# Recurrence gates of a two-layer hybrid block: plain float32 on dense 64x64 blocks in the four quarters of the array

## The chip, the cores and the metric

The kernel runs on one core of a Trainium2 chip. The metric is the device time of one launch, in microseconds (us). All weights are streamed from DRAM during the launch; the host only lays the inputs out.

## What is computed

Two layers work on 256 latent tokens and 256 context tokens (512 columns in all) of width 1024. Each layer normalises its input, sends it through three mixers (a recurrent block A, a gated linear recurrence B, neighbourhood attention C), merges these with gates, and adds a squared-ReLU MLP. The change is in A. Its recurrence needs two gates for each direction `d`; each is a product of the convolved input `xc` with a block-diagonal matrix, in blocks of 64 channels, cut here to what matters:

```python
xc = centred_depthwise_conv(x_in, conv_w, conv_b)            # (B, T, 512)
xb = xc.reshape(B, T, LRU_BLOCKS, LRU_BLOCK)                 # 8 blocks of 64
r = sigmoid(einsum('btni,dnio->dbtno', xb, wa) + ba)         # d = 2 directions
i = sigmoid(einsum('btni,dnio->dbtno', xb, wx) + bx)
log_a = -LRU_C * r * softplus(-lam)
a = exp(log_a); b = sqrt(-expm1(2 * log_a)) * (i * xc)
hf = linear_scan(a[0], b[0], h0f, False); hb = linear_scan(a[1], b[1], h0b, True)
y = (hf + hb) * gelu(gate_in)
```

## The kernel before

Tokens stand in columns, features in partitions. The kernel is a list of pieces: a piece is the products of one streamed 128x1024 weight tile (`raw`, split into a rounded part `whi` and the rest `wlo`, three products for one), and after every few products a piece yields. Between two yields the class `Lanes` issues steps of dependent chains: lane H (mixer B, `hgrn`), lane A (`attention`), lane L (`lru`, the recurrence of A), N and X (norm and modulation). A step names how many yields it waits. The framework then schedules the instructions of each engine by its own estimate of when their inputs are there; what it fixes is each engine's order, which is what the order rows below show.

For each of the four channel groups `j` of a layer the piece `ax` (tiles `pax`) gives the input of A, `fin_conv` makes `xc` of it, the piece `ag` (`pag`) gives the GeLU branch, and then `lru` starts. It splits the weights `gw` (128x512: four 128x128 matrices with zeros off the diagonal blocks) into `lw` and the input `xc` into `lx`, and multiplies three times for each gate:

```python
ws = [two_k("lw", F32R).rearrange("p (a b) -> p a b", b=P) for _ in range(2)]
split(*ws, gw)
split(*xs, xc)
def product(dst, i):
    for n, (a, b) in enumerate(((0, 0), (0, 1), (1, 0))):
        nc.tensor.matmul(dst, lhsT=ws[a][:, i, :], rhs=xs[b], start=(n == 0), stop=(n == 2))
```

So there are eight `lru` chains (two layers, four groups), each with two directions and two gates, `pr` and `pi`, and 512 columns in both layers. Both gates use the one PSUM bank of tag L. Tag H has two banks, which `hgrn` and every second call of `acc4` (the gates `pg` of the merge among them) take in turn. Tiles of 512 float32 come from a ring of 25 (`t2`), larger ones from a ring of 13 (`t4`). GpSimd's queue (POOL) issues the loads of `gw` and of the attention bias.

Other products use a part of the array at a time: `lv` (within `hgrn`) and `pav` (in `attention`) go to two column tiles of 64 in turn, in plain float32; `ada` goes to four column tiles of 32, in plain float32; the scores `sc` of the two heads go to two row tiles of 64, in float32r.

Of the kernel before, what the change touches and what calls it, by code (L numbers as in the profile page):

```python
# [11 lines left out]
F32R = mybir.dt.float32r  # L12
# [7 lines left out]
P = 128  # L20
# [7 lines left out]
HB = 64  # L28
NLEV = 6
# [27 lines left out]
def merge_order(l):  # L57
    # some gates first, while the mixers' chains end
    count = {}
    for part in MERGE[l].split():  # L60
        bi = int(part[0])
        for what in part[1:]:
            i = count.get((bi, what), 0)
            count[bi, what] = i + 1
            yield bi, BRANCH_ORDER[bi], {"g": "gate", "p": "proj"}[what], i
# [35 lines left out]
class Piece:  # L101
    """Products with streamed weights: body(weights) yields after each run of products."""
# [5 lines left out]
class Lanes:  # L108
    """Chains of dependent steps that are issued between the runs of products.

    A step yields the time that the vector engine needs for what it issued, and how many runs more the chain waits."""
# [43 lines left out]
def hybrid_kernel(  # L155
# [67 lines left out]
    def split(hi, lo, src, scale=None, eng=nc.vector):  # L223
        # hi <- rounded part of scale * src, lo <- the rest
# [21 lines left out]
    def mm3_pairs(dsts, ws, x, nk, c0, c1):  # L246
        # two pieces at a time, so that x may still be arriving
# [15 lines left out]
    def layer_scalars():  # L263
# [13 lines left out]
        for l in range(DEPTH):  # L277
            # f = lb + (1 - lb) * (1 + tanh) / 2 as offset and slope
# [40 lines left out]
    def rope_tables(l):  # L319
        # ctab[:, cos|sin, tile, k|q, head, :], with the norm's gains and the scores' scale  # L320
# [8 lines left out]
    mod = [cpool.tile([P, 3, 2, 16], F32, name=f"mod{l}") for l in range(DEPTH)]  # L329

    def modulation_rows():
        # most sections, a row for each feature: the vector engine has time while the tensor engine is busy
# [34 lines left out]
    def last_modulation():  # L367
        # the last section: four groups of columns in four parts of the array
# [55 lines left out]
    def column_sums(parts, n, tag="A"):  # L424
        # sums over the features, one column for each 128 tokens
# [12 lines left out]
    def spread(r, n, tag="A"):  # L438
        # a row of n * 128 columns in every partition
# [14 lines left out]
    def modulated(u, r, a, b, k, s):  # L454
        # u = h * r * a + b in high and low parts
# [29 lines left out]
    def small_rstd(ss, n, temps):  # L485
        # 1 / sqrt(ss / n + eps) for a few columns: a first guess from the exponent, two steps
# [6 lines left out]
        # with x = v * r * r: r * (15 - 10 x + 3 x^2) / 8, but for the factor 3 / 8, then r * (3 - x) / 2 with that factor  # L493
# [14 lines left out]
    def first_half():  # L508
        # the latent stream's norm, before its products are issued
        q_ = lanes.lanes["N"]  # L510
        while len(q_) > 1 and lanes.step("N"):
            pass

# [1 line left out]
    def hgrn(l, j, TF, Q, vtok, sog, ys):  # L515
# [4 lines left out]
        # products over blocks, states of the context stream  # L520
# [9 lines left out]
        # within blocks of 64 tokens, the blocks of a tile side by side  # L530
# [7 lines left out]
        def place(b, src, shift):  # L538
            # blocks in the upper (b = 0) or the lower half of the partitions
# [13 lines left out]
        def mixed(t, hh, c0, n):  # L553
            # [first halves of slot 0 | second halves of slot 1] of the 2*hh blocks in columns c0..c0+n
# [17 lines left out]
        # A^T[s, t] of both directions, level by level  # L572
        Tt = TF[:]
        width = T2
        for lev in range(8):
# [11 lines left out]
            # widen the products to blocks of 2*hh  # L587
# [30 lines left out]
        # final states of the context stream  # L618
# [18 lines left out]
        # outputs, token-major  # L637
# [34 lines left out]
    def attention(l, j, qk, vtok, bias, ys):  # L672
        Tq = T2 if l == 0 else TL
        misc = two_k("misc")
        # normalised keys and queries, token-major: [k | q] of two heads for each 128 tokens
# [23 lines left out]
        # rotary embedding of the latent tokens  # L699
# [48 lines left out]
        def softmax(qt, sc):  # L748
            # both heads at once
# [55 lines left out]
        def applied(qt):  # L805
            # both heads at once, in two parts of the array
# [28 lines left out]
    def lru(l, j, xc, ge, gw, ys):  # L835
# [3 lines left out]
        xs = [two_k("lx", F32R) for _ in range(2)]  # L839
        ws = [two_k("lw", F32R).rearrange("p (a b) -> p a b", b=P) for _ in range(2)]  # L840
        split(*ws, gw)
        split(*xs, xc)
        yield 1.2, 0

        def product(dst, i):
            for n, (a, b) in enumerate(((0, 0), (0, 1), (1, 0))):
                nc.tensor.matmul(dst, lhsT=ws[a][:, i, :], rhs=xs[b], start=(n == 0), stop=(n == 2))
        for d in range(2):
            c = 2 * j + d
            pr_ = psum("L", "pr")  # L850
            product(pr_, 2 * d)
            nc.scalar.activation(rr[:, d], pr_, AF.Tanh, bias=hb[l][0][:, c:c + 1], scale=0.5)
            yield
            pi_ = psum("L", "pi")
            product(pi_, 2 * d + 1)
            nc.scalar.activation(iis[d], pi_, AF.Tanh, bias=hb[l][1][:, c:c + 1], scale=0.5)
# [37 lines left out]
    def fin_query(Tq, Q, p_):  # L894
        # twice the silu
# [5 lines left out]
    def fin_outgate(l, Tq, sog, p_):  # L901
        # the gain over four times (1 + tanh)
# [17 lines left out]
    def fin_gelu(Tq, ge, p_):  # L920
        # twice the tanh GeLU
# [12 lines left out]
    def mixer_pieces(l):  # L934
        T = T2 if l == 0 else TL
        heads = []
        for j in range(4):
# [9 lines left out]
            def opened(nm, m=m, j=j):  # L947
                # tiles of a chain, when its first piece begins
# [613 lines left out]
```

## Time and profile before

| | |
|---|---|
| median of 3 runs | 1526.17 us (1525.85 to 1526.55) |
| the profiled execution's span | 1526.3 us |
| TensorE (PE) busy | 1513.7 us, 99% of the span |
| VectorE (DVE) busy | 1115.9 us, 73% |
| ScalarE (ACT) busy | 735.0 us, 48% |
| GpSimd (POOL) busy | 26.4 us, 2% |
| granted TensorE clock, mean | 0.999 of full |

The profile is of one execution; its span goes from the first to the last instruction and is its time as far as the page tells it. It lies within the three timed runs, 0.1 us over their median. Busy time of PE counts a product from its start to its modelled end, and products overlap, so the time that a product takes from the others is read from start to start in the timeline.

### The profile page before, as it was taken

The page shows a single profiled execution, that of the slowest core. Times are in us where ns is not written, and L with a number is a line of the kernel's source. Part 1 is how long each engine was busy: PE and PEld are TensorE (multiplying, and loading weights), DVE is VectorE, ACT ScalarE, POOL GpSimd, SP SyncE. Part 2 cuts the span into 40 slices and gives each one's busy share as a digit, 9 for nine tenths or more (in the row PEclk, how much of TensorE's full clock was granted, in tenths as well). Part 3 has the DMA queues.
Part 4 walks back from the last instruction along what each step waited for, and adds up shares of the span by engine and source line. Part 5 has one row for each costly group of instructions (what it writes and reads, how often), then busy time and mean ns, then how long its engine had stood idle before and what let it go on. Part 6 is the DMA issues. An engine that isn't in the chain of part 4 may idle for free.

```text
span 1526.3 us, 24145 instructions
## 1 busy us (share of the span) xinstructions
PE 1513.7 (99%) x9554; PEld 1300.8 (85%) x9554; DVE 1115.9 (73%) x2118; ACT 735.0 (48%) x1229; POOL 26.4 (2%) x57
## 2 busy tenths in 40 slices
PE   9999999999999999999999999999999999999999
PEld 4778788878888889888888889888888899999999
DVE  6776768586478898988685856778787856776664
ACT  3457575666333333532322323475766854454442
POOL 0200000020000000000000000000000000000000
PEclk9999999999999999999999999999999999999999
DMA  9413122221273562445463532313313345755553
GB/s 368 146 53 104 56 90 70 70 77 62 91 250 136 187 240 70 171 174 206 139 220 127 204 126 82 133 63 126 104 70 105 109 167 182 274 167 184 186 183 125
DMA packets 61793, 217.36 MB, mean 142 GB/s; under 512 B 7792, under 2 KB 9456, under 8 KB 61680
## 3 DMA queue, kind: packets, MB, share of 16 engines
q1 hardware_dynamic: 59328, 209.88, 39.5%
q0 software_dynamic: 1648, 5.77, 1.2%
q8 instruction: 75, 1.23, 0.3%
q14 instruction: 38, 0.31, 0.1%
q10 hardware_dynamic: 704, 0.17, 0.1%
HBM read 214.74 MB, written 1.05 MB: 141 GB/s over the span
## 4 chain that ended last, share of the span: by engine, by line
PE 96%; DVE 2%; ACT 1%; issue 1%; DMA 0%; SPq 0%; DVEq 0%
PE pd L240 7%; PE pd L242 7%; PE pd L241 7%; PE pf L242 5%; PE pf L240 5%; PE pf L241 5%; PE pg L240 5%; PE pg L241 4%; PE pg L242 4%; PE ptok L1027 3%; PE ptok L1029 3%; PE ptok L1028 3%; PE lv L547 2%; PE pp L241 2%; PE pp L240 2%; PE pp L242 2%
## 5 line engine op out<-in xcount | busy, mean ns | idle before, releaser
L226 ACT CAST whi<-raw 128x1024 fp32r<-128x1024 f32 x296 | 310.3, 1050 | 477.0 <-PE pd L241 157.2
L227 DVE TENSOR_TENSOR wlo<-raw,whi 128x1024 fp32r<-128x1024 f32 x295 | 360.3, 1223 | 151.2 <-ACT whi L226 149.4
L242 PE MATMUL pd<-hhi,wlo 128*128 128x256 f32 (+1 forms) x544 | 177.8, 327 | 0.0
L240 PE MATMUL pd<-hhi,whi 128*128 128x256 f32 (+1 forms) x544 | 177.8, 327 | 0.0
L241 PE MATMUL pd<-hlo,whi 128*128 128x256 f32 (+1 forms) x544 | 177.7, 327 | 0.0
L354 DVE CUSTOM_DVE_ANT_0 junk<-arow,crow 128x1024 bf16<-128x1024 f32 x144 | 173.3, 1219 | 2.2 <-DMA arow<-in_adaw 2.0
L241 PE MATMUL pf<-xlo,whi 128*128 128x256 f32 (+1 forms) x464 | 155.0, 334 | 0.0
L242 PE MATMUL pf<-xhi,wlo 128*128 128x256 f32 (+1 forms) x464 | 155.0, 334 | 0.0
L240 PE MATMUL pf<-xhi,whi 128*128 128x256 f32 (+1 forms) x464 | 155.0, 334 | 0.0
L240 PE MATMUL pg<-xhi,whi 128*128 128x512 f32 (+1 forms) x384 | 131.5, 342 | 0.0
L241 PE MATMUL pg<-xlo,whi 128*128 128x512 f32 (+1 forms) x384 | 129.2, 336 | 0.0
L242 PE MATMUL pg<-xhi,wlo 128*128 128x512 f32 (+1 forms) x384 | 129.2, 336 | 0.0
L1145 DVE SCALAR_TENSOR_TENSOR h<-pd,mod,h 128x256 f32<-128x256 f32 x120 | 54.9, 480 | 81.2 <-PE pd L242 79.2
L241 PEld LDWEIGHTS pd<-hlo,whi 128*128 128x128 f32 x544 | 103.5, 190 | 8.8
L240 PEld LDWEIGHTS pd<-hhi,whi 128*128 128x128 f32 x544 | 103.5, 190 | 8.8
L242 PEld LDWEIGHTS pd<-hhi,wlo 128*128 128x128 f32 x544 | 103.5, 190 | 8.6
L241 PEld LDWEIGHTS pf<-xlo,whi 128*128 128x128 f32 x464 | 88.1, 190 | 8.8
L242 PEld LDWEIGHTS pf<-xhi,wlo 128*128 128x128 f32 x464 | 88.1, 190 | 8.7
L240 PEld LDWEIGHTS pf<-xhi,whi 128*128 128x128 f32 x464 | 88.0, 190 | 8.7
L1027 PE MATMUL ptok<-whi,xhi 128*128 128x512 f32 (+1 forms) x224 | 87.4, 395 | 1.1 <-DVE h L1145 1.1
L1029 PE MATMUL ptok<-wlo,xhi 128*128 128x512 f32 (+1 forms) x224 | 84.4, 377 | 0.0
L1028 PE MATMUL ptok<-whi,xlo 128*128 128x512 f32 (+1 forms) x224 | 84.2, 376 | 0.2 <-DVE xlo L463 0.2
(329 smaller groups left out, 3240.0 us busy)
## 6 DMA issues: line engine op xcount, KB each, us to landing
raw<-in_wpack SPq DMA_DIRECT2D x296, 512.0 KB, 3.5
arow<-in_adaw SPq DMA_DIRECT2D x72, 512.0 KB, 4.7
a<-in_ada0w SPq DMA_DIRECT2D x16, 512.0 KB, 10.4
araw<-in_lastw SPq DMA_DIRECT2D x8, 512.0 KB, 6.3
bias<-in_biasd POOLq DMA_DIRECT2D x7, 512.0 KB, 4.3
h<-in_xT SPq DMA_DIRECT2D x4, 512.0 KB, 5.5
gw<-in_lruw POOLq DMA_DIRECT2D x8, 256.0 KB, 2.9
out<-h SPq DMA_DIRECT2D x8, 128.0 KB, 2.0
```

The costliest lines, as they stand in the source:

```text
L226: nc.scalar.copy(hi, src)
L227: eng.tensor_tensor(out=lo, in0=src, in1=hi.bitcast(F32), op=ALU.subtract)
L240: nc.tensor.matmul(d, lhsT=whi[:, k, :], rhs=xhi, start=(k == 0), stop=False)
L241: nc.tensor.matmul(d, lhsT=whi[:, k, :], rhs=xlo, start=False, stop=False)
L242: nc.tensor.matmul(d, lhsT=wlo[:, k, :], rhs=xhi, start=False, stop=(k == nk - 1))
L354: nc.vector.tensor_tensor_reduce(out=junk, in0=raw, in1=crow[s], scale=1.0, scalar=0.0, op0=ALU.mult, op1=ALU.add, accum_out=section_of(l, ...
L547: nc.tensor.matmul(dst, lhsT=lhs(b), rhs=rhs(b), start=True, stop=True)
L1027: nc.tensor.matmul(dst, lhsT=xhi[:, k, tsl], rhs=whi[:, kk, :], start=(k == 0), stop=False)
L1028: nc.tensor.matmul(dst, lhsT=xlo[:, k, tsl], rhs=whi[:, kk, :], start=False, stop=False)
L1029: nc.tensor.matmul(dst, lhsT=xhi[:, k, tsl], rhs=wlo[:, kk, :], start=False, stop=(k == KD - 1))
L1145: nc.vector.scalar_tensor_tensor(out=h[:, d, sl], in0=p_[:, sl], scalar=mods(l, section, s)[:, d:d + 1], in1=h[:, d, sl], op0=ALU.mult, op ...
```

## The change

The gate weights are stored as dense 64x64 blocks (`gw` is 128x256). Nothing is split any more: the products are plain float32. Each 64x64 block has a quarter of the array, by the partitions it is read from and those it writes to. For the second gate the host stores the two blocks with their halves changed over, so its input must be `xc` with the upper and lower 64 partitions exchanged; two DMAs on GpSimd's queue make that copy, `lxw`. A bank now holds half of each gate: `pr` (tag L) and `pi` (tag H) are two banks that are filled together, and four tanh of 64 partitions each empty them. Comments were taken out of the whole file as well, which is left out here.

```diff
+LB = 64
...
     def lru(l, j, xc, ge, gw, ys):
         Tq = T2 if l == 0 else TL
         rr, tau = four_k("lr"), four_k("ltau")
         iis = [two_k("li"), two_k("li")]
-        xs = [two_k("lx", F32R) for _ in range(2)]
-        ws = [two_k("lw", F32R).rearrange("p (a b) -> p a b", b=P) for _ in range(2)]
-        split(*ws, gw)
-        split(*xs, xc)
-        yield 1.2, 0
-
-        def product(dst, i):
-            for n, (a, b) in enumerate(((0, 0), (0, 1), (1, 0))):
-                nc.tensor.matmul(dst, lhsT=ws[a][:, i, :], rhs=xs[b], start=(n == 0), stop=(n == 2))
+
+        xw = two_k("lxw")
+        blk = slice(0, LB), slice(LB, P)
+        for b in range(2):
+            nc.gpsimd.dma_start(out=xw[blk[b]], in_=xc[blk[1 - b]])
+        yield 0.0, 2
+
+        def products(d, banks):
+
+
+            for b, p_ in enumerate(banks):
+                nc.tensor.matmul(p_[blk[b]], lhsT=gw[blk[b], 2 * d, :], rhs=xc[blk[b]], start=True, stop=True)
+                nc.tensor.matmul(p_[blk[1 - b]], lhsT=gw[blk[b], 2 * d + 1, :], rhs=xw[blk[b]], start=True, stop=True)
         for d in range(2):
             c = 2 * j + d
-            pr_ = psum("L", "pr")
-            product(pr_, 2 * d)
-            nc.scalar.activation(rr[:, d], pr_, AF.Tanh, bias=hb[l][0][:, c:c + 1], scale=0.5)
+            banks = psum("L", "pr"), psum("H", "pi")
+            products(d, banks)
+            for dst, g in ((rr[:, d], 0), (iis[d], 1)):
+                for b in range(2):
+                    o = blk[b ^ g]
+                    nc.scalar.activation(dst[o], banks[b][o], AF.Tanh, bias=hb[l][g][o, c:c + 1], scale=0.5)
             yield
-            pi_ = psum("L", "pi")
-            product(pi_, 2 * d + 1)
-            nc.scalar.activation(iis[d], pi_, AF.Tanh, bias=hb[l][1][:, c:c + 1], scale=0.5)
             nc.scalar.activation(tau[:, d], rr[:, d], AF.Tanh, bias=s8[l][1][:, c:c + 1], scale=s8[l][1][:, c:c + 1])
...
-                    m.gw = two_k("gw").rearrange("p (a b) -> p a b", b=P)
+                    m.gw = two_k("gw")[:, :4 * LB].rearrange("p (a b) -> p a b", b=LB)
...
-    lw = np.zeros((DEPTH, 4, P, 2, 2, P), np.float32)
+    lw = np.empty((DEPTH, 4, P, 2, 2, LB), np.float32)
...
+            rows = b ^ gi
+            lw[:, :, rows * LB:(rows + 1) * LB, :, gi] = w[:, :, :, b].transpose(0, 2, 3, 1, 4)
```

Line numbers differ between the two files (before L547, L746, L1027 to L1029 are L548, L747, L1032 to L1034 of the changed kernel). On PE in layer 0, group 0, first direction (`ptok` are the products of the next group's token piece, `sc` the attention scores), there stood before, with the second gate `pi` some 20 rows further on:

```order
L547 MATMUL lv<-QQ,km 64x64 x8
L1027 MATMUL ptok<-whi,xhi 128x512
L1028 MATMUL ptok<-whi,xlo 128x512
L1029 MATMUL ptok<-wlo,xhi 128x512
L1027 MATMUL ptok<-whi,xhi 128x512
L1028 MATMUL ptok<-whi,xlo 128x512
L1029 MATMUL ptok<-wlo,xhi 128x512
L746 MATMUL sc<-rotT 128x256 x6
L746 MATMUL sc<-kcT,qT 128x256 x6
L847 MATMUL pr<-lx,lw 128x512 x3
L1027 MATMUL ptok<-whi,xhi 128x512
```

Of the changed kernel, the same place:

```order
L548 MATMUL lv<-QQ,km 64x64 x8
L747 MATMUL sc<-rotT 128x256 x6
L747 MATMUL sc<-kcT,qT 128x256 x6
L1032 MATMUL ptok<-whi,xhi 128x512
L1033 MATMUL ptok<-whi,xlo 128x512
L1034 MATMUL ptok<-wlo,xhi 128x512
L1032 MATMUL ptok<-whi,xhi 128x512
L1033 MATMUL ptok<-whi,xlo 128x512
L1034 MATMUL ptok<-wlo,xhi 128x512
L851 MATMUL pr<-xc,gw 64x512
L852 MATMUL pr<-lxw,gw 64x512
L851 MATMUL pi<-xc,gw 64x512
```

The four products of a direction stand together here (the fourth, `pi<-lxw`, is the next row), between full-array products, and the scores moved ahead of the token products.

On PE in layer 1, group 0, first direction, there stood before, with the scores of each query tile in one run of 12 some rows further on:

```order
L547 MATMUL lv<-QQ,km 64x64 x4
L1027 MATMUL ptok<-whi,xhi 128x512
L1028 MATMUL ptok<-whi,xlo 128x512
L1029 MATMUL ptok<-wlo,xhi 128x512
L1027 MATMUL ptok<-whi,xhi 128x512
L1028 MATMUL ptok<-whi,xlo 128x512
L1029 MATMUL ptok<-wlo,xhi 128x512
L847 MATMUL pr<-lx,lw 128x512 x3
```

Of the changed kernel, the end of that stretch (the first of the four products, `pr<-xc`, stands 22 rows ahead of the second):

```order
L1032 MATMUL ptok<-whi,xhi 128x512
L747 MATMUL sc<-rotT 128x256 x3
L747 MATMUL sc<-kcT,qT 128x256
L747 MATMUL sc<-rotT 128x256 x3
L747 MATMUL sc<-kcT,qT 128x256 x5
L1033 MATMUL ptok<-whi,xlo 128x512
L1034 MATMUL ptok<-wlo,xhi 128x512
L1032 MATMUL ptok<-whi,xhi 128x512
L1033 MATMUL ptok<-whi,xlo 128x512
L1034 MATMUL ptok<-wlo,xhi 128x512
L852 MATMUL pr<-lxw,gw 64x512
L851 MATMUL pi<-xc,gw 64x512
```

One direction's four products are in two bursts here, and the scores of the two heads, one after the other before, come in mixed runs (four of one head, four of the other, then in turn).

On POOL's queue, from layer 0 on, there stood before one `gw` and one `bias` in turn. Of the changed kernel, the rows for the last group of layer 0 and the first two of layer 1:

```order
L327 TENSOR_TENSOR ctab<-cst,gf_74 128x64 x16
L973 DMA gw<-in_lruw 128x256
L844 DMA lxw<-xc 64x512 x2
L965 DMA bias<-in_biasd 128x1024
L973 DMA gw<-in_lruw 128x256
L965 DMA bias<-in_biasd 128x1024
L844 DMA lxw<-xc 64x512 x2
L973 DMA gw<-in_lruw 128x256
L965 DMA bias<-in_biasd 128x1024
L844 DMA lxw<-xc 64x512 x2
```

The two copies of a group are queued behind the loads for the next groups.

## Rows read from the trace of the kernel before

**Rows 1.** The page: span, busy time by engine, chain that ended last.

```profile
span 1526.3 us, 24145 instructions
...
PE 1513.7 (99%) x9554; PEld 1300.8 (85%) x9554; DVE 1115.9 (73%) x2118; ACT 735.0 (48%) x1229; POOL 26.4 (2%) x57
...
PE 96%; DVE 2%; ACT 1%; issue 1%; DMA 0%; SPq 0%; DVEq 0%
```

**Rows 2.** Waits of PE, all of nine: total us, times, longest.

```profile
PE pf L253 <- ACT xhi L462: 2.7, 3, 1.1
...
PE ptok L1028 <- DVE xlo L463: 0.2, 1, 0.2
```

**Rows 3.** Timeline of PE, 112.85 to 114 us: start, us, instruction, count.

```profile
113.08 0.85 PE L847 MATMUL pr<-lx,lw 128*128 128x512 f32 x3
113.77 0.39 PE L1027 MATMUL ptok<-whi,xhi 128*128 128x512 f32 x1
```

**Rows 4.** Timeline of PE around a run of `lv`, 101.3 to 103.1 us.

```profile
101.53 0.39 PE L1029 MATMUL ptok<-wlo,xhi 128*128 128x512 f32 x1
101.84 0.69 PE L547 MATMUL lv<-QQ,km 128*64 128x64 f32 x16
102.46 0.50 PE L1027 MATMUL ptok<-whi,xhi 128*128 128x512 f32 x1
102.79 0.39 PE L1028 MATMUL ptok<-whi,xlo 128*128 128x512 f32 x1
```

**Rows 5.** Timeline of PE around four products of `ada`, 24.4 to 25.9 us.

```profile
24.85 0.64 PE L1333 MATMUL ada<-a,cs 128*32 128x256 f32 x8
25.42 0.73 PE L998 MATMUL ptok<-whi,xhi 128*128 128x512 f32 x2
```

**Rows 6.** The same, only what runs between 24.85 and 24.88 us.

```profile
24.85 0.42 PE L1333 MATMUL ada<-a,cs 128*32 128x256 f32 x4
```

**Rows 7.** Timeline of PE around `pav` and the scores, 108 to 112 us.

```profile
108.85 1.90 PE L812 MATMUL pav<-PT,tok 128*64 128x256 f32 x16
110.68 0.97 PE L746 MATMUL sc<-kcT,qT 64*128 64x256 f32 x12
111.59 0.50 PE L1027 MATMUL ptok<-whi,xhi 128*128 128x512 f32 x1
```

**Rows 8.** Timeline of PE where one head's scores stand alone.

```profile
1197.31 0.62 PE L746 MATMUL sc<-rotT 64*128 64x256 f32 x3
1197.77 0.52 PE L746 MATMUL sc<-kcT,qT 64*128 64x256 f32 x3
1198.21 0.38 PE L240 MATMUL pg<-xhi,whi 128*128 128x256 f32 x1
```

**Rows 9.** Timeline of PE: the last product of `pax`, layer 1, group 0.

```profile
991.98 0.40 PE L242 MATMUL pax<-xhi,wlo 128*128 128x512 f32 x1
```

**Rows 10.** Timeline of DVE: the last step of `xc`, same group.

```profile
996.81 0.74 DVE L915 SCALAR_TENSOR_TENSOR xc<-xpre,prb,xc 128x510 f32<-128x510 f32 x1
```

**Rows 11.** DMA issues by line: queue, count, KB each, median us to landing.

```profile
bias<-in_biasd POOLq DMA_DIRECT2D x7, 512.0 KB, 4.3
...
out<-h SPq DMA_DIRECT2D x8, 128.0 KB, 2.0
```

**Rows 12.** Timeline of POOL: the bias of layer 1, group 3.

```profile
1097.57 0.54 POOL L960 DMA_DIRECT2D bias<-in_biasd  x1 [13.88 <-PE kt L623]
```

**Rows 13.** Timeline of DVE: the last step of `xc`, layer 1, group 2.

```profile
1121.69 0.74 DVE L915 SCALAR_TENSOR_TENSOR xc<-xpre,prb,xc 128x510 f32<-128x510 f32 x1
```

**Rows 14.** Instructions of tile `lx`: ns min/median/max, first and last start.

```profile
L226 ACT CAST lx<-xc x8: 602/636/642, 94.6 to 1185.6; 128x512 fp32r<-128x512 f32 x8
L227 DVE TENSOR_TENSOR lx<-xc,lx x8: 673/685/689, 95.4 to 1189.0; 128x512 fp32r<-128x512 f32 x8
```

**Rows 15.** Instructions of tile `pr`, and who waited for it.

```profile
L852 ACT ACTIVATE lr<-pr,hba x16: 687/690/703, 99.2 to 1203.8; 128x512 f32<-128x512 f32 x16
...
  ACT lr L852: 12.1, 7
```

More of the change, by code (lines that the diff above doesn't have):

```diff
@@ L1490, in _lay @@
     a["prm"] = pm
-    lw = np.zeros((DEPTH, 4, P, 2, 2, P), np.float32)
+    lw = np.empty((DEPTH, 4, P, 2, 2, LB), np.float32)
     for gi, nm in enumerate(("lru_wa", "lru_wx")):
-        w = f[nm].reshape(DEPTH, 2, 4, 2, 64, 64)
+        w = f[nm].reshape(DEPTH, 2, 4, 2, LB, LB)
         for b in range(2):
-            lw[:, :, b * 64:(b + 1) * 64, :, gi, b * 64:(b + 1) * 64] = w[:, :, :, b].transpose(0, 2, 3, 1, 4)
-    a["lruw"] = lw.reshape(DEPTH, 4, P, 4, P)
+            rows = b ^ gi
+            lw[:, :, rows * LB:(rows + 1) * LB, :, gi] = w[:, :, :, b].transpose(0, 2, 3, 1, 4)
+    a["lruw"] = lw.reshape(DEPTH, 4, P, 4, LB)
     r = np.arange(4)
```

## Prediction

> **What bounds the kernel now.** I read the page first. PE is busy for 99% of the span and has 96% of the chain that ended last [rows 1], so the time is what the products take one after another. The waits of PE come next: nine in all, 2.7 us the largest line and about 9 us together, at the start and the norms, none at the gates [rows 2]. DVE and ACT wait for PE instead; the tanh behind `pr` waited 12.1 us [rows 15]. So an edit counts by what it does to the sequence on PE, or if it makes PE wait. Busy times of PE overlap, so I take durations from start to start in the timeline, between neighbours. The profiled execution's span, 1526.3 us, is the time against which I make the sum; the runs' median is 0.1 us less, which I neglect.
>
> **What the change removes on PE.** Three products of a gate take 113.77 - 113.08 = 0.69 us [rows 3], 0.684 with the unrounded starts. There are 2 layers x 4 groups x 2 directions x 2 gates = 32 such threes: -21.9 us. They use the whole array, like the stream around them, and cost nothing on the way in or out.
>
> **What it adds on PE: the products.** A plain float32 product has two records. `pav` shows it: eight products, 16 records, and the scores start 1.83 us behind its start [rows 7]. The two column tiles run side by side, so these are 8 steps; less 0.1 for the way out, one pass of 256 columns takes 0.216 us. With four tiles, four products of `ada` take 0.57 us until the next full product [rows 5], and four of their eight records begin within 0.03 us [rows 6]. So tiles of one shape run side by side, the first passes of all and then the second ones. For 512 columns a pass is 0.432 us, and a burst of up to four quarters 0.864 us. No row shows a 64x64 tile, nor plain float32 on 64 rows. The bounds are 0.43 us (one pass would do) and 2.15 us (below); I take 0.864, since `ada` and `pav` differ from it only in the tile's width, and two row tiles run side by side too: twelve score products take 0.91 us [rows 7], six of one head alone 0.90 us [rows 8].
>
> In PE's new order eleven of the sixteen directions have their four products together. In five (groups 1 and 2 of layer 0; 0, 1 and 2 of layer 1) something stands between the first, which reads `xc`, and the second, which reads the copy. That makes 21 bursts: 21 x 0.864 = +18.1 us. Products together: -3.8 us.
>
> **What it adds on PE: changes of shape.** Between the last full product before a run of `lv` and the second one behind it lie 102.79 - 101.53 = 1.26 us [rows 4]. In it are two ordinary steps of 0.23 (0.69 / 3, [rows 3]) and eight of `lv`; at 64/256 of 0.216 these are 0.43 in all, in the unrounded starts 0.46. What is left, 0.34 to 0.37 us, is the price of leaving the full array and coming back, half of it a change. The two tails show it: `lv` starts 0.31 behind a product whose step is 0.23, and the first product behind takes 0.33. I take 0.165 us a change, bounds 0.15 to 0.185. The Trainium skill, "TensorEngine Tiling (Array Packing)", section Key Properties, says that changing the tiling mode, not just the tile, drains the engine. Here the trace agrees and gives the drain its price; without it the sum would be 6.3 us less.
>
> Going through PE's order in both kernels, with the shape of each product known from the code (full, two column tiles, four column tiles, two row tiles, quarters), I count 201 changes before and 239 after. The quarters are a new shape, and the schedule cuts other runs around them. 38 x 0.165 = +6.3 us (5.7 to 7.0).
>
> **What it moves on PE.** In layer 1 the scores of the two heads no longer alternate throughout; runs of one head leave half the array empty. Counted in steps (two neighbours on different row tiles are one), 126 become 147. A step is 0.117 us: six alone take 0.90 with about 0.2 for the way in [rows 8]. 21 x 0.117 = +2.5 us, or nothing if the second tile's products start ahead of the first's. Runs of `pav` that are cut need two more steps of two passes: +0.9 us. The runs of `lv` come out even.
>
> **What costs nothing.** ACT loses two casts a group (0.636 each) and DVE two subtractions (0.685) [rows 14]; ACT gains four tanh a group, at most 0.69 each [rows 15], 12 us in all. PE hardly waits for either [rows 2], so I book no gain and no loss.
>
> The copy `lxw` starts when `xc` is done: 997.55 us, where the last `pax` product streamed until 992.2 [rows 9, 10], so 5.3 us behind. Two issues of 0.54 [rows 12] and a landing of 2.0 to 4.3 us (no row shows a copy within SBUF; the bounds are a 128 KB store and a 512 KB load [rows 11]; I take 3) end it 8.5 to 10.8 us behind `pax`. In PE's order, stepped through with the durations above, the first product that reads it comes 12.6 us behind `pax` at the earliest, in groups 1 and 2 of layer 1, and over 16 us in layer 0. So it is hidden, with 1.8 us to spare in the worst case; without that cover each us late in eight groups costs 8 us. POOL's queue stands in order, so the copy also waits behind `bias` and `gw` of later groups. In layer 1 group 3's bias was issued at 1097.6 us [rows 12], and group 2's `xc`, whose copy is behind it in the new queue, was ready only at 1122.4 [rows 13], 25 us later. Halved `gw` loads and three ring tiles fewer can only help.
>
> **Sum.** -21.9 + 18.1 + 6.3 + 2.5 + 0.9 = +5.9 us: 1526.3 + 5.9 = 1532.2 us. With the bounds of the small terms it goes from +2.9 to +6.6, and new waits of a few us on top make the forecast's own range 1529 to 1537.
>
> **Rivals.** The measurement tells 0.2% from no change, 3 us.
>
> *Products on quarters don't run side by side (slower).* Two at a time, a whole group takes 1.73 us and a group of three the same: 16 x 0.86 = +13.8, 1546 us. Against it stand the rows of column and of row tiles; for it, that none shows both at once. Worse would be strict order with the two passes of a product next to each other: a second pass then holds back the product behind it until the first has gone, eight passes take five steps, 2.15 us, a group of three four steps, 11 x 1.29 + 5 x 0.86 = +18.5, 1550.7 us. That four of eight records begin together [rows 6] speaks against it. The Trainium skill, "TensorE: Matmul & The Clock Gate", section Part 3 (The mechanism), says that matmuls start in strict program order, from which this would follow; by that rule alone the time would be 1550.7 us.
>
> *A wait for the second bank (slower).* `pi` now takes one of tag H's two banks in each direction until its tanh are done, 4 x 0.69 = 2.8 us with those of `pr`. The next but one user of H, an `lv` or a `pg`, waits for that on PE, with all the products queued behind it. It decides if ACT is more than some 3 us late; 1 us in each of 16 directions would give 1548 us. Against it: ACT is 48% busy [rows 1] and mostly waits itself.
>
> *The cuts cost less (no change).* If row tiles start ahead of their turn (scores at nothing) and a change next to quarters costs half, as the rest of the array may go on: -3.8 + 0.9 + 38 x 0.08 = +0.1, 1526.4 us.
>
> *Plain float32 on 64 rows takes one pass (faster).* Then a burst is 0.43 and the sum 21 x 0.43 = 9.1 lower: -3.2, 1523 us, and 1520.6 if the scores cost nothing; a burst under 0.55 decides it, with the other terms as forecast. For it speaks only that no row shows the form; every plain float32 run of the trace has two records a product.
>
> **Chances and range.** Forecast 0.47; cuts cost less 0.18; one pass 0.16; two at a time 0.06; strict order 0.04; the bank 0.09. Faster is the one pass, 0.16; same the cheap cuts, 0.18; slower the other four, 0.66. The time is the forecast's, 1532.2. The range goes down to 1522, which takes in most of the one pass's case, and up to 1546, which takes in two quarters at a time: about 0.15 is left out.
>
> **What would show it.** The timeline of PE at the gates: four first records of `pr` and `pi` within 0.03 us, the second ones 0.43 behind, and about 0.86 us for a burst; eight first records spread over 1.3 us or more would show the first rival, a single record for each product the last. The step from a burst to the second full product behind it shows the change's price. The waits of PE should list neither `lxw` nor a bank of H for more than a few us. The gate lines' share, the `sc` runs in layer 1 and the spans of the two layers' mixers show where the rest went: layer 0's mixers about 2 us longer, layer 1's about 4. The prediction is wrong above all if PE's order does not set the time as I step through it, or if a quarter streams at another rate.

## The result, and the profile after

The changed kernel takes 1542.82 us (median of 4 runs, 1541.85 to 1546.13), the kernel before 1526.36 us (median of 4, 1525.85 to 1528.69): a ratio of 1.0105 (95% interval 1.0091 to 1.0118), 16.5 us slower. The forecast was 5.9 us slower.

The page of the profile after answers to [rows 1]:

```profile
span 1544.3 us, 24258 instructions
...
PE 1524.4 (99%) x9585; PEld 1292.7 (84%) x9586; DVE 1103.9 (71%) x2102; ACT 746.1 (48%) x1245; POOL 35.5 (2%) x73
...
PEclk8999999999999999999999999999999999999999
...
PE 92%; ACT 4%; DVE 3%; issue 1%; DMA 0%; SPq 0%; DVEq 0%; ACTq 0%
```

PE is still busy for 99%, but of the chain that ended last it has 92%, where it had 96%; ACT and DVE now have 7% of it. The waits of PE, answering to [rows 2] (total us, times, longest), are fourteen instead of nine and 16.5 us instead of 9.1. New are these:

```profile
PE lv L586 <- DVE QQ L599: 3.5, 3, 1.6
...
PE tp L794 <- ACT s L770: 1.6, 3, 0.5
...
PE lv L548 <- ACT li L860: 0.8, 1, 0.8
...
PE tp L794 <- ACT s L786: 0.7, 1, 0.7
PE ptok L1032 <- ACT sog L908: 0.5, 1, 0.5
```

None names the copy `lxw`. Only the third is the new bank of tag H (`li` is what the tanh of the second gate write); the others are attention (`tp` transposes the softmax `s`), `hgrn` (`QQ` for `lv`) and its output gate.

The gates themselves, timeline of PE at the first direction of layer 0, group 0, answering to [rows 3]:

```profile
100.44 0.39 PE L1034 MATMUL ptok<-wlo,xhi 128*128 128x512 f32 x1
100.76 0.64 PE L851 MATMUL pr<-xc,gw 64*64 64x512 f32 x1
100.77 0.64 PE L852 MATMUL pr<-lxw,gw 64*64 64x512 f32 x1
100.77 0.64 PE L851 MATMUL pi<-xc,gw 64*64 64x512 f32 x1
100.78 0.64 PE L852 MATMUL pi<-lxw,gw 64*64 64x512 f32 x1
101.24 0.59 PE L851 MATMUL pr<-xc,gw 64*64 64x512 f32 x1
...
101.78 0.50 PE L1032 MATMUL ptok<-whi,xhi 128*128 128x512 f32 x1
102.11 0.39 PE L1033 MATMUL ptok<-whi,xlo 128*128 128x512 f32 x1
```

Four first passes begin within 0.02 us, the second ones 0.48 us behind. From the product ahead to the second one behind lie 1.67 us; less two ordinary steps of 0.228 that is 1.21 us for a burst with its way in and out.

Where a direction is cut, in layer 0, group 1:

```profile
178.31 0.40 PE L1034 MATMUL ptok<-wlo,xhi 128*128 128x512 f32 x1
178.64 1.07 PE L851 MATMUL pr<-xc,gw 64*64 64x512 f32 x2
179.64 0.66 PE L794 MATMUL tp<-con,s 128*128 128x128 f32 x4
180.22 0.64 PE L852 MATMUL pr<-lxw,gw 64*64 64x512 f32 x1
...
181.24 0.55 PE L794 MATMUL tp<-con,s 128*128 128x128 f32 x3
```

One product alone (two passes, one row "x2") takes 1.00 us to the next instruction, the three behind it 1.02. A quarter alone costs what four cost together.

The copy, instructions of tile `lxw` (ns min/median/max, first and last start) and its landing, answering to [rows 11, 12]:

```profile
L844 POOL DMA_DIRECT2D lxw<-xc x16: 520/524/536, 88.7 to 1203.7; - x16
...
DMA to landing us min/median/max: 2.2/2.2/3.1
```

Where the time went, by the starts of the same products in both traces: the profiled execution of the changed kernel was 2.5 us late when the first gate was still to come (first `pag` at 82.29 us, before 79.77). In its first 40 us the mean granted clock was 0.87, in the other trace 0.96, so more of them went by at the lower of the two levels, 1.2 GHz; that belongs to this execution, and its own time, 1546.13, is 3.3 us over the median. From there to the first `pp`, the end of layer 0's mixers and gates, 8.5 us are lost (390.47 became 401.53), none in layer 0's MLP, 7.0 in layer 1's mixers (`pp` at 1255.85 became 1273.94), and nothing behind it. So the change itself lost 15.6 us in this trace: 7.0 are waits of PE, 8.6 lie in PE's own sequence, where the profile lists no idle time between the products.

### The profile page after: what moved, and what is told of

Its sections match the earlier page's. It is cut to its first block, busy times and chain, and to the rows that moved or that the text cites. A ratio compares the mean times of both kernels' runs of the same rounds, so it can differ in the third digit from the quotient of the medians.

```text
span 1544.3 us, 24258 instructions
## 1 busy us (share of the span) xinstructions
PE 1524.4 (99%) x9585; PEld 1292.7 (84%) x9586; DVE 1103.9 (71%) x2102; ACT 746.1 (48%) x1245; POOL 35.5 (2%) x73
## 3 DMA queue, kind: packets, MB, share of 16 engines
HBM read 213.69 MB, written 1.05 MB: 139 GB/s over the span
## 4 chain that ended last, share of the span: by engine, by line
PE 92%; ACT 4%; DVE 3%; issue 1%; DMA 0%; SPq 0%; DVEq 0%; ACTq 0%
PE pd L241 7%; PE pd L243 7%; PE pd L242 7%; PE pf L241 5%; PE pf L243 5%; PE pf L242 5%; PE pg L241 4%; PE pg L242 4%; PE pg L243 4%; PE ptok L1032 3%; PE ptok L1033 2%; PE ptok L1034 2%; PE pp L242 2%; PE pp L243 2%; PE pp L241 2%; PE lv L548 2%
## 5 line engine op out<-in xcount | busy, mean ns | idle before, releaser
L1032 PE MATMUL ptok<-whi,xhi 128*128 128x512 f32 (+1 forms) x224 | 89.7, 402 | 1.6 <-DVE h L1150 1.1
L1034 PE MATMUL ptok<-wlo,xhi 128*128 128x512 f32 (+1 forms) x224 | 84.6, 377 | 0.0
```

The source lines that it names most:

```text
L1032: nc.tensor.matmul(dst, lhsT=xhi[:, k, tsl], rhs=whi[:, kk, :], start=(k == 0), stop=False)
L1034: nc.tensor.matmul(dst, lhsT=xhi[:, k, tsl], rhs=wlo[:, kk, :], start=False, stop=(k == KD - 1))
```

## Experiments

The theory after the result (A, the order): the loss beyond the products comes from a line that the forecast had not priced, the first step of the chain: `yield 1.2, 0` had become `yield 0.0, 2`. The class `Lanes` reads the first number as work for the vector engine and holds other chains back by it:

```python
cost, more = next(q[0]) or (0.0, 0)
self.load += cost
self.next[lane] = self.now + max(SPACING[lane], self.load / CAPACITY + 1) + more
...
if self.next[lane] <= self.now and (self.load <= LIMIT or lane in "NX") and self.step(lane):
```

The rivals: B, the copy and the four tanh; C, the second bank. Counts of changes of shape and of bursts in the expectations are read from each kernel's order on PE, as in the forecast.

**old_step.** The changed kernel with the step of before:

```diff
-        yield 0.0, 2
+        yield 1.2, 0
```

> The changed kernel with the first step of the recurrence's chain as before: a declared cost of 1.2 and no extra wait, in place of 0.0 and 2. Theory A (the order): what was lost beyond the products comes from this step, which regroups TensorE's order and puts the chains of ScalarE and VectorE against each other. In the new order the changes of shape go from 239 to 220 (19 x 0.165 = 3.1 us less), the bursts of quarters from 21 to 18 (3 x 0.864 = 2.6 us less), the scores of the two heads alternate again (2.5 us less), and the 7 us of new waits shrink: 1542.8 less 8 to 15, 1528 to 1535. Rival B (the copy and the four tanh): the first product that reads the copy now stands 10.5 us behind the input's products instead of 11.9, the copy becomes late: 1541 to 1550, with the copy among the waits of TensorE. Rival C (the second bank): the two banks are as before, so nothing changes but the bursts: 1538 to 1543.

Measured: 1533.32 us against 1527.62, ratio 1.0032 (1.0020 to 1.0044), by the ratio 4.9 us slower than before. About 11 of the 16 us hang on that line. B and C expected none of it. The copy is not waited for although its first reader comes earlier. The waits of PE that are left and new:

```profile
PE tp L794 <- ACT s L786: 2.2, 2, 1.2
...
PE ptok L1032 <- ACT sog L908: 0.8, 1, 0.8
```

**no_copy.** The changed kernel without the copy; the second gate reads the input itself, so it does not compute the same gates:

```diff
...
-        for b in range(2):
-            nc.gpsimd.dma_start(out=xw[blk[b]], in_=xc[blk[1 - b]])
...
-                nc.tensor.matmul(p_[blk[1 - b]], lhsT=gw[blk[b], 2 * d + 1, :], rhs=xw[blk[b]], start=True, stop=True)
+                nc.tensor.matmul(p_[blk[1 - b]], lhsT=gw[blk[b], 2 * d + 1, :], rhs=xc[blk[b]], start=True, stop=True)
```

> The changed kernel without the copy: no DMA, and the second gate reads the input itself, so its two halves take each other's channels. The order on TensorE is the same but for one change of shape (238 for 239), the cut bursts too. A (the order): within 2 us of the changed kernel, 1541 to 1545. B (the copy): the waits go and with them half the loss or more, 1528 to 1536. C (the second bank): as A.

Measured: 1543.91 us, ratio 1.0097 (1.0080 to 1.0114), the same as the changed kernel. The copy costs nothing. The directions are also cut in the same places (one product, a `tp`, three products), so the copy's arrival is not what cut them.

**banks.** The kernel before with both gates issued together, in two banks:

```diff
-            pr_ = psum("L", "pr")
-            product(pr_, 2 * d)
-            nc.scalar.activation(rr[:, d], pr_, AF.Tanh, bias=hb[l][0][:, c:c + 1], scale=0.5)
+            banks = psum("L", "pr"), psum("H", "pi")
+            for i, p_ in enumerate(banks):
+                product(p_, 2 * d + i)
+            for i, dst in enumerate((rr[:, d], iis[d])):
+                nc.scalar.activation(dst, banks[i], AF.Tanh, bias=hb[l][i][:, c:c + 1], scale=0.5)
             yield
-            pi_ = psum("L", "pi")
-            product(pi_, 2 * d + 1)
-            nc.scalar.activation(iis[d], pi_, AF.Tanh, bias=hb[l][1][:, c:c + 1], scale=0.5)
```

> The kernel before, with both gates of a direction issued together into two banks (tags L and H) as in the change; the products are still three of the full array for each gate, the step as before. A (the order): TensorE has the same products and 191 changes of shape instead of 201, 1.7 us less; 1523 to 1527. C (the second bank): the next users of tag H wait for the tanh, 1530 to 1542. B: 1525 to 1528.

Measured: 1528.17 us, ratio 1.0006 (0.9997 to 1.0015), no difference. PE waits for the second bank once:

```profile
PE lv L547 <- ACT li L854: 0.2, 1, 0.2
```

C is out. The time lies above the range that A gave: ten changes of shape fewer, 1.7 us by their price, need not appear in it. By the starts of the same products layer 1's mixers are 1.7 us shorter than before and layer 0's 1.8 longer.

**new_step_before.** The kernel before, only its step changed:

```diff
+        yield 0.0, 2
         xs = [two_k("lx", F32R) for _ in range(2)]
         ws = [two_k("lw", F32R).rearrange("p (a b) -> p a b", b=P) for _ in range(2)]
         split(*ws, gw)
         split(*xs, xc)
-        yield 1.2, 0
```

> The kernel before, with the changed kernel's step (cost 0.0, wait 2) ahead of the splits and no step behind them; nothing else is touched, the products are the same. A (the order): 215 changes of shape instead of 201 (2.3 us more), runs of gates cut in 42 for 34, other runs displaced, and chains that meet: 3 to 12 us slower, 1529 to 1538. B and C: no copy and no second bank, so 1525 to 1528.

Measured: 1534.80 us, ratio 1.0041 (1.0026 to 1.0056), 6.3 us slower by the ratio, with the same products, no copy and one bank. No wait of PE is new against [rows 2], and the largest is the same:

```profile
PE pf L253 <- ACT xhi L462: 2.7, 3, 1.1
```

So this loss lies in PE's sequence. Its trace is 0.6 us ahead of the kernel before when layer 0's mixers end and 5.4 behind at the last `pp`, so layer 1's mixers lost 6.0 us. From each start to the next, the scores take 2.4 us more there, `pav` 1.5 and the token products `ptok` around them 2.1, which makes up the 6.0: it is the attention's runs that are cut. Counted from the first `pag` on, layer 0 lost 0.9. Another 1.5 us of this trace belong to the clock: behind a wait of 1.1 us at the start of layer 1's MLP, which the kernel before has too, the mean granted clock is 0.86 over 11.8 us (part of them at 1.2 GHz), where before it is 1.00 and the same products take 10.3 us.

The second set asks where the 4.9 us of `old_step` are. A2: the four tanh of 64 partitions in a row. D: the products and shapes on PE. The place in question, timeline of ACT in `old_step`, layer 0, group 1:

```profile
192.31 0.68 ACT L860 ACTIVATE lr<-pr,hba 64x512 f32<-64x512 f32 x1 [0.33 <-PE pi L852]
193.01 0.69 ACT L860 ACTIVATE li<-pr,hbx 64x512 f32<-64x512 f32 x1
193.60 0.67 ACT L860 ACTIVATE lr<-pi,hba 64x512 f32<-64x512 f32 x1
194.29 0.69 ACT L860 ACTIVATE li<-pi,hbx 64x512 f32<-64x512 f32 x1
...
199.62 1.28 ACT L778 ACT_TABLE_LOAD   x1
...
206.75 1.71 ACT L786 ACTIVATE s<-s,misc 128x256 f32<-128x256 f32 x4 [1.26 <-DVE misc L782]
```

and on PE, same kernel, a bit later:

```profile
205.73 0.39 PE L1033 MATMUL ptok<-whi,xlo 128*128 128x512 f32 x1
207.31 0.84 PE L794 MATMUL tp<-con,s 128*128 128x128 f32 x4 [1.19 <-ACT s L786]
```

A tanh of 64 partitions takes the 0.69 us that one of 128 took [rows 15], so the four take 2.7 us where one gate's took 0.69. The table load for the softmax came at 197.70 in the trace of before and comes at 199.62 here; the softmax's last step came at 202.93 and comes at 206.75, and PE stands for 1.2 us.

**two_tanh.** `old_step` with whole banks (the loop over halves is gone):

```diff
-                for b in range(2):
-                    o = blk[b ^ g]
-                    nc.scalar.activation(dst[o], banks[b][o], AF.Tanh, bias=hb[l][g][o, c:c + 1], scale=0.5)
+                nc.scalar.activation(dst, banks[g], AF.Tanh, bias=hb[l][g][:, c:c + 1], scale=0.5)
```

> The changed kernel with the old step (1533.3 us, 4.9 us over the kernel before), and two tanh of 128 partitions for each direction in place of four of 64; each bank is taken whole, so that the two gates have one half exchanged. Theory A2 (the tanh): four tanh of 0.69 in a row, 2.7 us where one of 0.7 stood, make the softmax and the copies behind them late, and TensorE waits for these (3.9 us of new waits in old_step). With two the waits shrink to 1 us or less, and three changes of shape go: 1529 to 1530.5. Rival D (the products): what is left of the loss lies in the bursts, the changes of shape and the cut runs of the attention's products on TensorE, whatever ScalarE does: 1532 to 1534.

Measured: 1530.03 us against 1527.71, ratio 1.0015 (1.0005 to 1.0025), within what A2 gave. The wait of `tp` shrinks from 2.2 to 0.8 us, that of `sog` from 0.8 to 0.5:

```profile
PE tp L794 <- ACT s L786: 0.8, 2, 0.4
PE ptok L1030 <- ACT sog L906: 0.5, 1, 0.5
```

These are 1.3 us of new waits where `old_step` has 3.0 by its two lines above (the expectation has 3.9), so 1.7 us less. By the starts of the same products, from the first `pag` to the last `pp`, `old_step` lost 5.1 us against before and `two_tanh` 0.9: more than half of the gain is not in the listed waits. A part of it is in layer 1, where three runs of `pav` with the same records are 0.5 us shorter each, `old_step` first:

```profile
1024.97 2.42 PE L813 MATMUL pav<-PT,tok 128*64 128x256 f32 x16
1027.33 0.44 PE L1032 MATMUL ptok<-whi,xhi 128*128 128x384 f32 x1
...
1021.10 1.90 PE L813 MATMUL pav<-PT,tok 128*64 128x256 f32 x16
1022.92 0.44 PE L1030 MATMUL ptok<-whi,xhi 128*128 128x384 f32 x1
```

In the long run the first two products start 0.27 us apart, in the short one 0.007.

**late_second.** `old_step` with the second gate's two tanh behind the yield, as before the change:

```diff
-            for dst, g in ((rr[:, d], 0), (iis[d], 1)):
+            def tanh(dst, g):
                 for b in range(2):
...
+            tanh(rr[:, d], 0)
             yield
+            tanh(iis[d], 1)
```

> The changed kernel with the old step, where the two tanh of the second gate are issued behind the yield, as before the change; the products stay together. A2: the softmax and its neighbours are no longer behind four tanh in a row, 1.4 us less in front of them, and half the new waits go: 1529.5 to 1532. D: 217 changes of shape for 220 and one burst less, 1 to 1.5 us less, 1531.5 to 1533. A third way: both banks are held longer, so the products of the second direction or an lv wait for the tanh: 1534 to 1540.

Measured: 1528.25 us, ratio 1.0002 (0.9992 to 1.0011), no loss that the ratio can tell, and more gained than A2 gave it. The medians hold executions whose mean granted clock is 0.995 to 1.0, up to 5 us apart; of those at 1.0 alone, seven of `late_second` have a median of 1528.1 us, three of `two_tanh` 1527.3, two of `old_step` 1531.2 and six of the kernel before 1526.0 (five beside `old_step` 1526.3). So some 2 us remain of the 4.9, and 1.2 with `two_tanh`: the two are not ranked, and these edits to the tanh were worth about 3 to 4 us. In the timeline of ACT the softmax is ahead of the second gate's tanh again:

```profile
192.28 0.68 ACT L860 ACTIVATE lr<-pr,hba 64x512 f32<-64x512 f32 x1 [0.33 <-PE pi L852]
192.99 0.68 ACT L860 ACTIVATE lr<-pi,hba 64x512 f32<-64x512 f32 x1
...
198.46 1.28 ACT L778 ACT_TABLE_LOAD   x1
...
203.25 0.68 ACT L860 ACTIVATE li<-pr,hbx 64x512 f32<-64x512 f32 x1
203.95 0.68 ACT L860 ACTIVATE li<-pi,hbx 64x512 f32<-64x512 f32 x1
204.54 1.70 ACT L786 ACTIVATE s<-s,misc 128x256 f32<-128x256 f32 x4
```

The last step of the softmax comes at 204.54, 2.2 us earlier, and no `tp` waits. But 2.0 us of other new waits stand there (`sog` 0.8, `PT` 0.7, `gt` 0.5), and the long runs of `pav` are still there, so of some 3 us gained about 1 is in the listed waits. Three changes of shape and a burst fewer came along in both kernels, some 0.5 to 1.5 us of the gain. That the tanh hurt through the waits alone, as A2 has it, is not shown: their order moved PE's sequence too.

**row_tiles.** `old_step` with one product for each block, whose 128 output columns are its two gates:

```diff
...
-                nc.tensor.matmul(p_[blk[b]], lhsT=gw[blk[b], 2 * d, :], rhs=xc[blk[b]], start=True, stop=True)
-                nc.tensor.matmul(p_[blk[1 - b]], lhsT=gw[blk[b], 2 * d + 1, :], rhs=xw[blk[b]], start=True, stop=True)
+                lhsT = gw[blk[b], 2 * d:2 * d + 2, :].rearrange("p a b -> p (a b)")
+                nc.tensor.matmul(p_, lhsT=lhsT, rhs=xc[blk[b]], start=True, stop=True)
...
-                    nc.scalar.activation(dst[o], banks[b][o], AF.Tanh, bias=hb[l][g][o, c:c + 1], scale=0.5)
+                    nc.scalar.activation(dst[blk[b]], banks[b][blk[g]], AF.Tanh, bias=hb[l][g][blk[b], c:c + 1], scale=0.5)
```

> The old step, and each block as one product on a row tile of 64x128: its two gates are the 128 output columns, the input is read in place, and there is no copy; two of the four tanh write to the other half of the partitions. Two passes of 512 as before, on two row tiles instead of four quarters; 219 changes of shape for 220, 18 bursts. If two row tiles stream as four quarters do, and the copy costs nothing: 1532 to 1535, the same as old_step. If the copy or the quarters had a price of their own on TensorE (B): 1526 to 1530. If a tanh that writes to the other half takes longer: 1536 or more.

Measured: 1533.69 us, ratio 1.0041 (1.0026 to 1.0056), no different from `old_step`. Two products do what four and a copy did, in the same time as far as the runs tell; a burst takes 1.06 us to the next instruction, mostly, where the four quarters take 1.02. Half of the tanh write to the other half of the partitions; of these two lines (ns min/median/max) the second does:

```profile
L856 ACT ACTIVATE lr<-pr,hba x16: 667/681/687, 97.9 to 1208.1; 64x512 f32<-64x512 f32 x16
L856 ACT ACTIVATE li<-pr,hbx x16: 686/687/690, 102.4 to 1210.7; 64x512 f32<-64x512 f32 x16
```

**row_split.** `row_tiles` with split input and weights, three products of one pass:

```diff
...
+        split(*ws, gw)
+        split(*xs, xc)
...
+            for n, (a, s) in enumerate(((0, 0), (0, 1), (1, 0))):
+                for b, p_ in enumerate(banks):
+                    nc.tensor.matmul(p_, lhsT=ws[a][blk[b], 2 * d:2 * d + 2, :].rearrange("p a b -> p (a b)"), rhs=xs[s][blk[b]], start=(n == 0), stop=(n == 2))
```

> As row_tiles, with the input and the weights split as before and three products of one pass for each block: 3 x 0.228 = 0.684 us for a burst instead of 0.864 to 0.96. 18 bursts x 0.18 to 0.28 = 3.2 to 5 us less; 233 changes of shape for 219, 14 x 0.165 = 2.3 us more; ScalarE and VectorE get the splits back. A2 and D alike: 1529 to 1533; if the splits make the softmax late (A2 more strongly), 1533 to 1538. It would beat the kernel before only if the changes of shape cost less beside the scores, 1525 to 1527.

Measured: 1533.60 us, ratio 1.0043 (1.0027 to 1.0059). The burst is shorter, as this timeline of PE shows (98.18 to 98.96, 0.78 us with the way out, right behind scores of the same shape). But there are 14 changes of shape more than in `row_tiles`, and the new waits of PE stay at 3.8 us (`row_tiles` has 3.7): 2.1 for `tok`, 1.0 for `s` among them. It is not the casts that stand in front of `tok`: in layer 1, group 0, three of the four tanh run on ACT from 1019.89 to 1021.98, and the copy to `tok` follows at 1022.01.

```profile
98.18 0.39 PE L853 MATMUL pr<-lx,lw 64*128 64x512 f32 x1
...
98.64 0.39 PE L853 MATMUL pr<-lx,lw 64*128 64x512 f32 x1
98.96 0.50 PE L1032 MATMUL ptok<-whi,xhi 128*128 128x512 f32 x1
```

The third set takes the step apart, asks whether the two causes add up, and tries for a better kernel.

**cost_only** and **wait_only.** The changed kernel with `yield 0.0, 0`, and with `yield 1.2, 2`:

```diff
-        yield 0.0, 2
+        yield 0.0, 0
```

> The changed kernel with the step 0.0, 0: the extra wait of 2 is taken out, the declared cost of nothing stays. Which half of the step does the harm? If the cost (the chains are issued as if the vector engine had nothing to do, so others come along at the same yields): 244 changes of shape and 22 bursts, more than the change's own 239 and 21, 1540 to 1546. If the wait: as old_step, 1531 to 1534.

> The changed kernel with the step 1.2, 2: the declared cost as before the change, the extra wait of 2 kept. If the cost did the harm: 224 changes of shape and 20 bursts for 220 and 18 of old_step, 1 to 2.5 us more than it, 1531 to 1536. If the wait did it: 1539 to 1545.

Measured: 1543.05 us, ratio 1.0099 (1.0077 to 1.0122), and 1534.19 us, ratio 1.0047 (1.0033 to 1.0061), against 1526.97. The declared cost does it: with 0.0 the loss is that of the change, with or without the extra wait, with 1.2 it is near that of `old_step`. In `cost_only` the largest of the new waits is there as in the changed kernel:

```profile
PE lv L586 <- DVE QQ L599: 3.5, 3, 1.6
```

**late_new_step.** `late_second` with the change's own step:

```diff
-        yield 1.2, 0
+        yield 0.0, 2
```

> The changed kernel with its own step 0.0, 2, and the two tanh of the second gate behind the yield as in late_second. If the two causes add up, the late tanh gives back the 3 to 5 us here too that it gave back with the old step: 1538 to 1540. If the tanh only hurt in the old order, or the order decides alone: 241 changes of shape and 22 bursts for 239 and 21, 1542 to 1544.

Measured: 1538.76 us, ratio 1.0074 (1.0053 to 1.0094). By the ratios the loss falls from 1.05% to 0.74%, 4.7 us, and by the runs at clock 1.0 from 15.7 us (1541.93) to 12.1 (1538.30, against 1526.24), 3.6 us, about what the late tanh gave with the old step. Here the gain is in the waits: of new ones the changed kernel has 7.0 us and this one 3.0. The largest has all but gone, so it hung on the tanh too:

```profile
PE lv L586 <- DVE QQ L599: 0.3, 1, 0.3
```

The two causes add up, although the order has two changes of shape and one burst more than the change.

**late_row_split.** `row_split` with the tanh of `late_second`.

> row_split with the tanh of the second gate behind the yield. If these were the harm there too, it gains what late_second gained on old_step, 3 to 5 us: 1528 to 1530.5, no faster than the kernel before. It beats that kernel only if more waits go than the 3.8 us which row_split shows at the attention's products and its token piece: 1523 to 1526.

Measured: 1531.22 us, ratio 1.0021 (1.0011 to 1.0032), 3.2 us slower; 3.4 us of the 6.6 that `row_split` lost are back, and PE no longer waits for `tok`. No version here beats the kernel before.

## Why the prediction was right or wrong

The direction was right, the size was not: 5.9 us forecast, 16.5 measured. The 1542.8 us lie outside the 1529 to 1537 that the forecast gave for itself. They lie within its wide range only because that went up to 1546 to take in two quarters at a time, which the trace rules out; that is luck. The forecast saw layer 0's mixers about 2 us longer and layer 1's about 4; they are 8.5 and 7.0 us longer.

**The products: the sum right, its parts not.** 0.864 and two changes of 0.165 were forecast for a burst, 1.19 us together; 1.21 is measured. The second passes start 0.48 us behind the first, not 0.43; two such steps leave 0.25 of the 1.21 for the way in and out, not 0.33, so two errors nearly cancel. Three rivals are settled: two at a time, strict order, and one pass. The rule of the Trainium skill, "TensorE: Matmul & The Clock Gate", section Part 3 (The mechanism), that matmuls start in program order, would, if the two passes of a product stand next to each other there, have put the second pass of the first product ahead of the next product; the trace does not agree, four first passes start within 0.02 us and the second ones 0.48 behind. At 1.21 us a whole burst is 0.16 cheaper than the two threes that it replaces (2 x 0.684), and a cut direction, two bursts, is dearer. `late_second`, with 17 bursts (20.6 us for the 21.9 removed), shows what the gates are worth when most of the rest is put right: no gain, or a loss of some 2 us.

**Changes of shape: there, but not priced by themselves.** "TensorEngine Tiling (Array Packing)", section Key Properties of the Trainium skill, names the drain, and this trace agrees that a change costs time: the last full product takes 0.32 us to the burst's start and the first behind it 0.33, where a step is 0.23, as around `lv` [rows 4]. What more of a change lies within the burst cannot be told from its passes here.

**Scores and `pav`: about right.** From start to start within runs the scores take 16.8 us where they took 14.7 (2.5 forecast), `pav` 16.3 where it took 15.1 (0.9 forecast). That speaks against the cheap cuts, in which the scores cost nothing. The forecast's terms of PE's sequence make 5.9, the trace 8.6; the 2.7 us between are not assigned to one term.

**The copy and the bank: right.** Landing 2.2 us where 3 was assumed, no wait for it, and no difference without it. The second bank costs 0.8 us, far from the 1 us a direction of its rival.

**"What costs nothing": this step failed.** It booked the new tanh at nothing, since PE hardly waited for ACT or DVE in the trace of before [rows 2]; the bank's rival leaned on ACT being 48% busy. What counts is what stands in ACT's order ahead of the instruction that PE needs next, not ACT's load: four tanh in a row stand in front of the softmax. The new waits are 7.0 us; the forecast had "a few us" of them outside its sum. `two_tanh`, `late_second` and `late_new_step` put the tanh's part at 3 to 4 us. With the change's own step it is in the waits (4.0 us fewer in `late_new_step`); with the old step 1 to 2 us of it are, and the rest is in PE's sequence.

**What was not priced: the step.** The forecast read its consequences on PE from the new order, the cuts, the changes of shape, the mixed scores, and counted them as if they came with the quarters. They came with `yield 0.0, 2`: some 11 us of the 16.5 go with it, and it costs 6 us in the kernel before too. In layer 1 it costs the same in both kernels, 5.8 us (7.0 less the 1.2 of `old_step`) and 6.0; in layer 0 it costs 4.7 us with the quarters (8.5 less 3.9) and 0.9 without. The declared cost was true, VectorE has nothing to split any more; but it also kept other chains from being issued at the same yields. How a smaller number leads the framework to cut the runs of gates, where the copy is not the reason, stays open.

**The base.** An execution's time is 1.8 us over its span (1546.13 and 1544.3), so the profiled execution of before was not within the runs shown but near 1528; the forecast had them equal. The ratio is not touched.

## What to carry to other kernels

In a kernel whose chains are interleaved by declared costs, a changed cost is a change of the whole order: try it by itself, with the products untouched, before a loss or a gain is put down to the products. An engine that is half idle is not free where the instruction that the bound engine needs next stands behind the new ones: look for what is queued there, in that stage, and not at its share of the span. Packing products into parts of the array pays a way in and out each time; here a burst of quarters took 1.21 us with both, the two threes in its place 1.37, and what was left was not enough to pay for the directions that were cut and for what moved around them.

## What the runs showed of the hardware

- A 64x64 product in plain float32 takes two passes for 512 columns, the second 0.48 us behind the first, alone or with three others: 1.00 us to the next instruction for one, 1.02 for three or four.
- Two row tiles of 64x128 take 1.06 us to the next instruction in most bursts, four quarters of 64x64 1.02; the times of the kernels do not differ (`row_tiles` and `old_step`, 1533.7 and 1533.3 us).
- Sixteen records of `pav` on two column tiles take 1.82 us to the next product where the first two start 0.007 us apart (`two_tanh`), and 2.36 where they start 0.27 apart (`old_step`).
- A tanh of 64 partitions takes as long as one of 128 (0.682 and 0.690 us), and as long where it writes to the other half of the partitions (0.687).
- The clock of the first 40 us differs from execution to execution: the mean granted clock is 0.96 in the trace of before and 0.87 in that of the change, whose first `pag` comes 2.5 us later. It can also fall later: in `new_step_before` it is 0.86 over 11.8 us behind a wait of 1.1 us, while the same wait in the trace of before leaves it at 1.00.
